# Where the matmul operands lie in SBUF: a 32-byte offset between stationary and moving tiles in a transformer block

## The chip, the cores and the metric

The kernel runs on one core of one Trainium2 chip. The metric is device time in microseconds (us) for one execution of the whole program; lower is better. Engines are named as in the profile: PE is TensorE (matmuls), PEld its weight loads, DVE VectorE, ACT ScalarE, POOL GpSimd, SP SyncE, which issues most DMAs. A matmul has a *stationary* operand (loaded into the array ahead of the matmul, the PEld rows) and a *moving* operand (streamed through it); both are read from SBUF, the result goes to PSUM.

## The reference

One layer of a streaming encoder on x of shape (1, 1024, 1024), float32:

```python
x = x + 0.5 * swiglu(rmsnorm(x, ffn1_norm), ffn1_w_gate, ffn1_w_up, ffn1_w_down)   # D_FF = 2816
h = rmsnorm(x, mix_norm); p = h @ w_in
#   A: gMLP spatial gating (8 groups x 64), B: gated DeltaNet (4 heads x 128), chunks of 64
x = x + concat(A, B) @ w_out
x = x + 0.5 * swiglu(rmsnorm(x, ffn2_norm), ffn2_w_gate, ffn2_w_up, ffn2_w_down)
y = rmsnorm(x, final_norm)
# swiglu(x, g, u, d) = (silu(x @ g) * (x @ u)) @ d
```

## The kernel before, in words

**Precision.** Every large product is made from float32r matmuls. `split` (line 60) makes two tiles of a float32 tile: a rounded one, `h` (a cast on ACT), and the remainder, `l` (a subtraction on DVE). `mm3` (line 55) then issues three matmuls into one PSUM bank: h x h, h x l, l x h, with the third argument pair as the moving operand. Small products in the mixer are plain float32 matmuls, transposes too.

**The two FFNs** (`ffn`, line 173) use Winograd's form of Strassen's scheme: seven products in place of eight on half-size blocks. `Combos` (line 107) holds the transposed activations and their sums (B11, B21, B22, T1 to T4), made once per FFN; they are the moving operands. For each of the 22 chunks of 128 hidden columns, `load_gu` (line 182) loads the gate and up weights, makes the weight sums on POOL and splits them into seven tiles of the pool `gp` (tag `gsp`); these are the stationary operands. `gu` (line 246) runs 7 products x 4 slices x 3 matmuls = 84 matmuls with 512 moving columns, and DVE and ACT combine the results; the hidden activations go to DRAM. Chunk 0 is done without the scheme by `gu_plain` (line 230) in two halves of 256 columns; a quarter of its products has as moving operand the tile B12, which comes from `gp` like the weights.

**Down projection.** Three `group`s (line 309) do the same on hidden activations and down weights: `group(0, 1)` has one pair of chunks per block, the other two have two. POOL and DVE make the sums in the buffers `hx`; `unit` (line 303) splits a left and a right factor into one tile (tag `cmb` of the pool `bp`, three buffers), and `mms` (line 335) runs 24 matmuls on it: the left factor is stationary, the right one moving. DVE adds finished banks into the residual `x` or into `acc`. The generator keeps two units prepared ahead of the one that runs. The last pair of chunks, number 10, goes without the scheme (`pair`, line 407, and the loop at line 435): 96 matmuls, both operands in `cmb` tiles.

**The mixer** (`middle`, line 659) projects `hT`, the transposed normalized activations in `actT` tiles of the pool `ap`. `proj_steps` (line 833) has the weights (`wk`, pool `wp`) stationary and `hT` moving, 512 columns; `token_steps` (line 694) has `hT` stationary and the weights moving, 256 or 264 columns of a 256- or 272-column slice. The steps of these generators are woven between the small products of the DeltaNet scan. Then `w_out` (line 555) has the transposed mixer output `yT` (pool `ap`) stationary and the weights (tag `gsp`) moving, 256 columns.

**Layout of SBUF.** Tiles of a pool lie one after another in the order of first use, `bufs` of each tag, rounded up to 32 bytes; a pool begins where the one opened before it ends. The pools that live throughout are `cp` (constants), `sm` (small statistics, three buffers for each of 11 tags, four for `ms` and `rs`), `xp` and `ap`; `gp`, `qp`, `bp` or the mixer's pools follow, by stage. In bytes from the start of a partition, before: `cp` 16,512, `sm` 21,152, `xp` 22,464, `ap` 55,232, and 120,768 for the first pool of a stage. `half` is 32 bytes and `grow` 4,096, so `grow` begins at 17,056, 32 past a multiple of 64. All tiles that a matmul reads begin at a multiple of 64.

```python
u = bp.tile([P, 2, 2, 2, 512], F32R, tag="cmb", name="unit", bufs=3)          # line 304
mm3(ps[t], u[:, 0, 0, j, tsl], u[:, 1, 0, j, tsl], u[:, 0, 1, j], u[:, 1, 1, j], ...)   # line 339
```

Of the kernel before, what the change touches and what calls it, by code (L numbers as in the profile page):

```python
# [10 lines left out]
F32 = mybir.dt.float32  # L11
F32R = mybir.dt.float32r
# [5 lines left out]
P = 128  # L18
# [12 lines left out]
def block_kernel(ctx: ExitStack, tc, a, out):  # L31
    nc = tc.nc

    def pool(stack, name, bufs=1, space=None):
        kw = {} if space is None else {"space": space}
        return stack.enter_context(tc.tile_pool(name=name, bufs=bufs, reuse_waits="tile", **kw))


    cp = pool(ctx, "cp")
    sm = pool(ctx, "sm", 3)  # L40
    xp = pool(ctx, "xp", 8)
    ap = pool(ctx, "ap", 4)
    dr = pool(ctx, "dr", 1, DRAM)

    ident = cp.tile([P, P], F32, tag="ident", name="ident")
    half = cp.tile([P, 8], F32, tag="half", name="half")
    nc.vector.memset(half, -0.5)

    def bank(p, tag):
        return p.tile([P, 512], F32, tag=tag, name=tag)  # L50

    def mm(*args, **kw):
        nc.tensor.matmul(*args, **kw)  # L53

    def mm3(o, lh, ll, rh, rl, first, last, **kw):
        mm(o, lh, rh, start=first, stop=False, **kw)
        mm(o, lh, rl, start=False, stop=False, **kw)
        mm(o, ll, rh, start=False, stop=last, **kw)

    def split(h, l, src):  # L60
        nc.scalar.copy(h, src)  # L61
        nc.vector.tensor_tensor(l, src, h, op=ALU.subtract)  # L62

    def grow(name):
        g = cp.tile([P, D], F32, tag="grow", name="grow")
        nc.scalar.dma_start(g, a[name].to_broadcast([P, D]))
        return g

    def rpow(o, i, w):
        nc.gpsimd.tensor_tensor(o, i, half[:, :w], op=ALU.pow)  # L70
# [9 lines left out]
    def normed(xt, g, xn, junk=None):  # L80
        rs = rstd_of(xt, xn if junk is None else junk, D)
        nc.vector.scalar_tensor_tensor(xn, xt, rs, g, op0=ALU.mult, op1=ALU.mult)  # L82
        return xn
# [5 lines left out]
    def acts():  # L89
        return [[act_tile() for _ in range(2)] for _ in range(2)]  # L90
# [7 lines left out]
    def to_T(pp, blk, tt, dst):  # L98
        sl = slice(tt * P, tt * P + P)
        for q in range(2):  # L100
            pv = transposed(pp, lambda i: blk(q * 4 + i))
            nc.scalar.copy(dst[q][:, 0, :, sl], pv)  # L102
            nc.vector.tensor_tensor(dst[q][:, 1, :, sl], pv, dst[q][:, 0, :, sl], op=ALU.subtract)
# [65 lines left out]
    def together(*parts, n=None):  # L169
        for _ in islice(zip_longest(*parts), n):  # L170
            pass

    def ffn(cb, wgu, wd, ps, gp, qp, bp, start, emit, before={}):
# [127 lines left out]
                nc.sync.dma_start(x[:, 1, ks], wd[2 * q:2 * q + 2][:, :, dh * 512:dh * 512 + 512].rearrange("j p n -> p j n"))  # L301

        def unit(l, r):
            u = bp.tile([P, 2, 2, 2, 512], F32R, tag="cmb", name="unit", bufs=3)
            for i, s in enumerate((l, r)):
                split(u[:, 0, i], u[:, 1, i], s)
            return u

        def group(p0, m, first, last):
            n = 2 * m  # L310
# [24 lines left out]
            def mms(ps, u, first, last, evac):  # L335
                for t in range(4):
                    tsl = slice(t * P, t * P + P)
                    for j in range(2):
                        mm3(ps[t], u[:, 0, 0, j, tsl], u[:, 1, 0, j, tsl], u[:, 0, 1, j], u[:, 1, 1, j],
                            first and j == 0, last and j == 1, skip_group_check=True)  # L340
                    if evac is not None:
                        evac(t, ps[t])
# [27 lines left out]
            def p1(kp, ks):  # L370
                u = unit(x1[:, 0, ks], x1[:, 1, ks])
                s1, t1 = st[kp]
                sub(x1[:, 0, ks], s1, x1[:, 0, ks], eng=other)
                sub(x1[:, 1, ks], x4[:, 1, ks], t1)
                return u
# [18 lines left out]
            ps = None  # L394
            for f, pp, start, stop, ev in plan:
                for kp in range(m):
                    def prep(f=f, kp=kp):
                        return f(kp, slice(2 * kp, 2 * kp + 2))

                    def run(u, pp=pp, kp=kp, start=start, stop=stop, ev=ev):  # L400
                        nonlocal ps
                        if start and kp == 0:
                            ps = [bank(*pp) for _ in range(4)]
                        mms(ps, u, start and kp == 0, stop and kp == m - 1, ev if kp == m - 1 else None)
                    yield prep, run
# [15 lines left out]
        for prep, run in units:  # L421
            ahead.append((run, prep()))
            if len(ahead) > 2:
                r, u = ahead.pop(0)
                r(u)
        prep = pair(10)
        r, u = ahead.pop(0)
        r(u)
        w = [prep(0)]
        r, u = ahead.pop(0)  # L430
# [4 lines left out]
        for t in range(8):  # L435
            tsl = slice(t * P, t * P + P)
            for f in range(2):
                fs = slice(f * 512, f * 512 + 512)
                p = bank(*X)
# [12 lines left out]
    def psums(stack, n):  # L452
        return [pool(stack, f"ps{i}", k, PSUM) for i, k in enumerate(n)]
# [5 lines left out]
    def load_x(src, ts):  # L459
        xs = {}  # L460
        for t in ts:
            xs[t] = xp.tile([P, D], F32, tag="x", name="x")
            nc.sync.dma_start(xs[t], src[t])
        return xs
# [6 lines left out]
    with ExitStack() as f1:  # L471
        ps = psums(f1, (4, 4))
        gp = pool(f1, "gp")
        qp = pool(f1, "qp")
        bp = pool(f1, "bp")
        cb = Combos(g, qp, bp)

        def start1(f):
            def xi(i):
                return xs[i], xs[i + 4]  # L480

            uv = [cb.sums() for _ in range(2)]
            for j in range(2):
                for i in range(2):
                    normed(xi(i)[j], g, xi(i)[j], uv[i][j])
            def b12():
                return [f.gtile(F32R, "B12").rearrange("p s (k n) -> p s k n", k=2) for _ in range(2)]

            weights = f.load_gu(0, True)
            next(weights)  # L490
            b = b12()
            parts = [cb.blocks(i, f.X, xi(i), uv[i], b) for i in range(2)]
            together(*parts, n=2)
            together(*parts, weights, n=2)
            xs.update(load_x(xdram, (2, 3, 6, 7)))
            f.gu_plain(slice(0, 256), b)
            rest = xi(2) + xi(3)
            ms = sm.tile([P, 4], F32, tag="ssk", name="ms4")
            for i, x in enumerate(rest):
                nc.scalar.activation(f.gtile(F32, "junk").rearrange("p s n -> p (s n)"), x, AF.Square, accum_out=ms[:, i:i + 1])  # L500
            rs = sm.tile([P, 4], F32, tag="rk", name="rs4")
            nc.vector.tensor_scalar(rs, ms, 1.0 / D, EPS, op0=ALU.mult, op1=ALU.add)
            rpow(rs, rs, 4)
            for i, x in enumerate(rest):
                nc.vector.scalar_tensor_tensor(x, x, rs[:, i:i + 1], g, op0=ALU.mult, op1=ALU.mult)
            together(*parts)
            b = b12()
            parts = [cb.blocks(i, f.X, xi(i), cb.sums(), b, eng=nc.vector) for i in range(2, 4)]
            together(*parts, n=4)
            f.gu_plain(slice(256, 512), b)  # L510
            together(*parts)

        st = {}

        def after(xts):
            st["gm"] = grow("mix_norm")
            xts.update(load_x(xdram, range(8)))

        def to_mid(t, xt):
            nc.sync.dma_start(xd[t], xt)  # L520
            if t == 0:
                st["hT"] = acts()
                st["xn"] = bp.tile([P, 4, D], F32, tag="cmb", name="xn", bufs=3)
            xn = st["xn"][:, t % 4]
            normed(xt, st["gm"], xn)
            return lambda: to_T((ps[1], "ax"), lambda c: xn[:, c * P:(c + 1) * P], t % 4, st["hT"][t // 4])

        ffn(cb, a["f1gu"], a["f1wd"], ps, gp, qp, bp, start1, to_mid, {2: [after]})
        hT = st["hT"]

    g2 = grow("ffn2_norm")
    with ExitStack() as mid:
        ps_m, ps_a, ps_s = psums(mid, (3, 2, 1))
        wp = pool(mid, "wp")
        ep = pool(mid, "ep")
        ts = pool(mid, "ts")
        up = pool(mid, "up")
        tl = pool(mid, "tl")
        lv = pool(mid, "lv")
        kp = pool(mid, "kp")  # L540
        yblk = middle(tc, nc, a, locals())

    with ExitStack() as f2:
        ps = psums(f2, (4, 4))
        bp = pool(f2, "bp")
        gp = pool(f2, "gp")
        qp = pool(f2, "qp")
        order = ((0, 4, 1, 5), (2, 6, 3, 7))
        yT = acts()
# [741 lines left out]
```

## Time and profile before

| | |
|---|---|
| median of 3 runs | 1914.35 us (1913.04 to 1918.01) |
| the profiled execution's own time | 1916.1 us |
| its span | 1914.0 us |
| PE busy | 1812.0 us, 95% of the span, 9,759 matmuls |
| mean granted TensorE clock | 0.981 |

The span is the time from the first to the last instruction of one profiled execution. Matmuls overlap, and the end of each is modelled, so the mean duration of a matmul in a row is longer than the distance from one start to the next; the pace is read from a piece with a count, as its length divided by the number. The chain of waits follows the work back from the last instruction; its pieces give start, length, engine, tile and line. A row of a group gives the shapes, the number of instructions, their busy time, the mean of one, and the idle time before them with what ended it.

### The profile page before, as it was taken

To read this page: it belongs to the slowest core of one execution; us is meant where nothing else is said; L and a number is where in the kernel's file an instruction comes from. 1 tells how busy PE (TensorE), PEld (TensorE's weight loads), DVE (VectorE), ACT (ScalarE), POOL (GpSimd) and SP (SyncE) were. 2 spreads that over 40 slices of the span, in tenths; PEclk is the share of its full clock that TensorE was granted. 3 is DMA by queue.
4 is the path that set the end of the run, shared out by engine and by line. 5 is a ranking of instruction groups with operands and counts; after the bars stand their busy time and mean duration, and the time that the engine had idled before them with its cause. 6 is when DMAs were issued, how large, how long until landed. Compare 5 with 4: busy or idle time off the path is not lost.

```text
span 1914.0 us, 25049 instructions
## 1 busy us (share of the span) xinstructions
PE 1812.0 (95%) x9759; PEld 1542.0 (81%) x9759; DVE 1253.3 (65%) x1663; ACT 674.2 (35%) x1171; POOL 665.9 (35%) x477
## 2 busy tenths in 40 slices
PE   6999999999798899898999999999999999979888
PEld 5888888887687689797788989988888888768766
DVE  7655555557988984668755236655555555798896
ACT  6333232334233343432354434433333332323233
POOL 4322222224647802221132402242323222454681
PEclk9999999999899999999999999999999999999999
DMA  6222222225222224354432343323232323531312
GB/s 227 92 91 78 88 78 89 77 89 200 89 79 97 84 107 141 122 182 122 130 90 65 118 145 122 115 74 97 68 99 67 99 67 98 171 115 57 119 44 88
DMA packets 95815, 199.98 MB, mean 104 GB/s; under 512 B 23857, under 2 KB 39505, under 8 KB 95697
## 3 DMA queue, kind: packets, MB, share of 16 engines
q1 hardware_dynamic: 93200, 193.95, 30.7%
q10 hardware_dynamic: 2496, 4.44, 0.8%
q8 instruction: 76, 1.25, 0.3%
q14 instruction: 43, 0.34, 0.1%
HBM read 149.06 MB, written 49.30 MB: 104 GB/s over the span
## 4 chain that ended last, share of the span: by engine, by line
PE 71%; DVE 15%; POOL 4%; issue 4%; ACT 3%; DMA 2%; DVEq 0%; POOLq 0%; SPq 0%; ACTq 0%
PE mm L53 40%; PE ax L53 29%; DVE unit L62 6%; DVE x L347 1%; POOL hx L323 1%; DVE acc L852 1%; POOL s L192 1%; PE sd L53 1%; DMA graw<-in_f1gu_dram 1%; PE ax L95 1%; PE sc L53 1%; POOL rs L70 0%; POOL E L778 0%; DVE xn L82 0%; ACT actT L102 0%
## 5 line engine op out<-in xcount | busy, mean ns | idle before, releaser
L53 PE MATMUL mm<-unit 128*128 128x512 f32 x960 | 240.9, 412 | 49.7 <-DVE acc L351 25.8
L62 DVE TENSOR_TENSOR unit<-hx,unit 128x1024 fp32r<-128x1024 f32 x128 | 247.2, 1971 | 45.0 <-ACT unit L61 44.3
L192 POOL TENSOR_TENSOR s<-graw 128x512 f32<-128x512 f32 x84 | 108.5, 1292 | 466.7 <-DMA graw<-in_f1gu_dram 178.9
L53 PEld LDWEIGHTS mm<-unit 128*128 128x128 f32 x960 | 192.0, 201 | 96.6 <-issue 48.9
L62 DVE TENSOR_TENSOR gs<-s,gs 128x512 fp32r<-128x512 f32 x168 | 162.0, 966 | 142.5 <-ACT gs L61 141.7
L61 ACT CAST unit<-hx 128x1024 fp32r<-128x1024 f32 x128 | 128.5, 1050 | 260.9 <-PE mm L53 84.7
L53 PE MATMUL ax<-unit 128*128 128x512 f32 x912 | 211.0, 390 | 4.0 <-DVE unit L62 3.4
L61 ACT CAST gs<-s 128x512 fp32r<-128x512 f32 x168 | 100.2, 620 | 317.9 <-POOL s L192 213.7
L53 PEld LDWEIGHTS ax<-unit 128*128 128x128 f32 x912 | 170.6, 188 | 40.6 <-DVE unit L62 4.2
L53 PE MATMUL ax<-T,gs 128*128 128x512 f32 x792 | 183.1, 389 | 0.0
L53 PEld LDWEIGHTS ax<-T,gs 128*128 128x128 f32 x792 | 148.7, 188 | 30.8
L62 DVE TENSOR_TENSOR ga<-graw,ga 128x512 fp32r<-128x512 f32 x134 | 96.2, 719 | 114.0 <-ACT ga L61 113.7
L53 PE MATMUL mm<-B,ga 128*128 128x512 f32 (+1 forms) x864 | 166.3, 347 | 0.2 <-ACT B L118 0.2
L53 PE MATMUL mm<-T,gs 128*128 128x512 f32 x720 | 166.4, 389 | 0.0
L53 PEld LDWEIGHTS mm<-T,gs 128*128 128x128 f32 x720 | 135.2, 188 | 28.0
L53 PEld LDWEIGHTS mm<-B,ga 128*128 128x128 f32 x864 | 139.7, 194 | 19.5 <-ACT B L118 0.5
L53 PE MATMUL mm<-actT,wk 128*128 128x512 f32 x576 | 152.3, 407 | 1.8 <-ACT ev L713 1.8
L53 PE MATMUL mm<-wk,actT 128*128 128x256 f32 (+1 forms) x1152 | 147.9, 286 | 0.0
L53 PEld LDWEIGHTS mm<-wk,actT 128*128 128x128 f32 x1152 | 141.2, 191 | 0.4
L53 PE MATMUL ax<-B,ga 128*128 128x512 f32 x528 | 126.9, 389 | 0.0
L323 POOL TENSOR_TENSOR hx<-hx 128x1024 f32<-128x1024 f32 x40 | 126.8, 3201 | 0.0
L53 PEld LDWEIGHTS mm<-actT,wk 128*128 128x128 f32 x576 | 105.0, 191 | 21.4 <-ACT ev L713 2.0
(240 smaller groups left out, 2756.4 us busy)
## 6 DMA issues: line engine op xcount, KB each, us to landing
graw<-in_f1gu_dram SPq DMA_DIRECT2D x44, 512.0 KB, 4.3
graw<-in_f2gu_dram SPq DMA_DIRECT2D x44, 512.0 KB, 3.9
hd<-sg SPq DMA_DIRECT2D x42, 512.0 KB, 5.1
hx<-hd SPq DMA_DIRECT2D x40, 512.0 KB, 6.3
hx<-in_f1wd_dram SPq DMA_DIRECT2D x20, 512.0 KB, 6.8
hx<-in_f2wd_dram SPq DMA_DIRECT2D x20, 512.0 KB, 7.4
x<-in_x_dram SPq DMA_DIRECT2D x16, 512.0 KB, 6.1
graw<-in_wo_dram SPq DMA_DIRECT2D x16, 512.0 KB, 3.8
```

Source lines behind the costliest of these rows:

```text
L53: nc.tensor.matmul(*args, **kw)
L61: nc.scalar.copy(h, src)
L62: nc.vector.tensor_tensor(l, src, h, op=ALU.subtract)
L95: nc.tensor.transpose(ps[:, i * P:(i + 1) * P], blk(i), ident)
L192: nc.gpsimd.tensor_tensor(f, u, v, op=op)
L323: eng.tensor_tensor(o, u, v, op=op)
L347: nc.vector.scalar_tensor_tensor(xv, p, 0.5, xv, op0=ALU.mult, op1=ALU.add)
L852: nc.vector.scalar_tensor_tensor(acc, pad[:, j:j + 512], cw[:, blk, j:j + 1], acc, op0=ALU.mult, op1=ALU.add)
```

## The change

All float32r stationary operands are meant to begin 32 bytes past a multiple of 64 and the moving ones at a multiple. A new helper, `shift`, takes a 32-byte tile at the start of a pool, which pushes what follows by 32 bytes; it is called for `gp` and `qp` in the first FFN, `wp` in the mixer, and `gp` in the second FFN. `unit` takes one flat tile of 4,112 elements in place of 4,096, with the right (moving) factor at its start and the left (stationary) one from element 2,056. To make room and keep `xp` and `ap` at a multiple of 64, `half` takes 64 bytes, and `sm` has two buffers per tag instead of three. `pair` and B12 are as before, and no instruction is added or taken away.

```diff
-    sm = pool(ctx, "sm", 3)
+    sm = pool(ctx, "sm", 2)
...
-    half = cp.tile([P, 8], F32, tag="half", name="half")
+    half = cp.tile([P, 16], F32, tag="half", name="half")[:, :8]
     nc.vector.memset(half, -0.5)
+
+    def shift(p):
+        p.tile([P, 8], F32, tag="shift", name="shift")
...
         def unit(l, r):
-            u = bp.tile([P, 2, 2, 2, 512], F32R, tag="cmb", name="unit", bufs=3)
-            for i, s in enumerate((l, r)):
-                split(u[:, 0, i], u[:, 1, i], s)
+            t = bp.tile([P, 4112], F32R, tag="cmb", name="unit", bufs=3)
+            u = [t[:, o:o + 2048].rearrange("p (s j n) -> p s j n", s=2, j=2) for o in (2056, 0)]
+            for v, s in zip(u, (l, r)):
+                split(v[:, 0], v[:, 1], s)
             return u
...
-                        mm3(ps[t], u[:, 0, 0, j, tsl], u[:, 1, 0, j, tsl], u[:, 0, 1, j], u[:, 1, 1, j],
+                        mm3(ps[t], u[0][:, 0, j, tsl], u[0][:, 1, j, tsl], u[1][:, 0, j], u[1][:, 1, j],
...
         gp = pool(f1, "gp")
+        shift(gp)
         qp = pool(f1, "qp")
+        shift(qp)
         bp = pool(f1, "bp")
...
         wp = pool(mid, "wp")
+        shift(wp)
...
         gp = pool(f2, "gp")
+        shift(gp)
         qp = pool(f2, "qp")
```

## The prediction

> **What bounds the kernel now.** I read the page's busy times first, then the chain of work that ended last, then the stretches of the span side by side, and last the timeline, for the pace of single matmuls. The page:
>
> ```profile
> span 1914.0 us, 25049 instructions
> PE 1812.0 (95%) x9759; PEld 1542.0 (81%) x9759; DVE 1253.3 (65%) x1663; ACT 674.2 (35%) x1171; POOL 665.9 (35%) x477
> PE 71%; DVE 15%; POOL 4%; issue 4%; ACT 3%; DMA 2%; DVEq 0%; POOLq 0%; SPq 0%; ACTq 0%
> ```
>
> TensorE is 71% of the chain that sets the end. The busy times by stretch (span, PE, weight loads, DVE, ACT, POOL; the granted clock third from the end) say where:
>
> ```profile
> 95.00:455.00 360.00, 360.00 (x1590) 298.20 (x1589) 196.77 (x263) 111.37 (x187) 92.50 (x73) 1.00 0.29 92
> 455.00:523.00 68.00, 55.04 (x228) 43.98 (x226) 64.29 (x51) 24.07 (x27) 43.90 (x16) 0.92 0.39 133
> 523.00:587.00 64.00, 64.00 (x270) 52.72 (x271) 50.95 (x45) 21.06 (x22) 22.86 (x8) 0.95 0.32 110
> 587.00:651.00 64.00, 50.24 (x212) 40.19 (x210) 62.81 (x36) 22.05 (x25) 61.08 (x22) 0.93 0.19 72
> 1090.00:1250.00 160.00, 154.74 (x1277) 151.42 (x1276) 82.22 (x143) 65.91 (x131) 37.32 (x38) 1.00 0.38 129
> 1296.00:1655.00 359.00, 359.00 (x1586) 297.36 (x1585) 196.32 (x263) 110.97 (x187) 92.18 (x72) 1.00 0.28 91
> ```
>
> The two gate/up loops (95 to 455, 1296 to 1655) are all TensorE at full clock, with DVE at 55%. In the down projection (455 to 700, and again from 1655) PE fills one stretch, and DVE and POOL fill those on both sides of it.
>
> Then the pace. The first two rows below are pieces of the chain of waits (start, us, engine, instructions); the others are timeline rows (start of the first to the modelled end of the last):
>
> ```profile
> 304.96 19.04 PE mm L53 x84
> 1191.87 43.31 PE mm L53 x361
> 727.93 6.95 PE L53 MATMUL mm<-wk,actT 128*128 128x264 f32 x56
> 1185.16 1.91 PE L95 MATMUL ax<-ident,x 128*128 128x128 f32 x16
> 1014.30 1.06 PE L53 MATMUL ax<-Z,ks 128*128 128x128 f32 x8
> ```
>
> A 512-column float32r matmul comes every 19.04 / 84 = 226.7 ns, a 256-column one every 43.31 / 361 = 120.0 ns. The difference, 106.7 ns for 256 columns, is 0.4167 ns per column; so each of them pays 120.0 - 106.7 = **13.3 ns beside its columns**, the same for both widths. This fixed part is all that the change can touch. Two things say that it need not be there. The plain float32 rows run at twice the time per column: 128 columns are 106.7 ns, and starts are about 109 ns apart for transposes ((1.91 - 0.27) / 15) and 112 ns for the products ((1.06 - 0.27) / 7), so they pay 2.3 and 5.3 ns, although each has a 128-column load of its own too. And it isn't constant: the 264-column matmuls come every (6.95 - 0.28) / 55 = 121.3 ns, where 264 x 0.4167 + 13.3 would be 123.3; they pay 11.3. Theirs are the only float32r operands whose slices start at steps other than whole multiples of 512 bytes (272 columns apart, 1,088 bytes). A cost that is paid once per load and gives way where the addresses or the phase shift looks like the weight load and the moving stream meeting in SBUF.
>
> **The change part by part.** It issues no instruction more or less, nothing is moved on a queue, and no DMA changes size. What changes is where tiles lie. Worked from the tile sizes: before, every matmul tile starts at a multiple of 64. After, `half` adds 32 bytes, `sm` loses 11 x 32 = 352, `xp` starts at 22,144 (64 x 346), `ap` at 54,912 (64 x 858), and the first pool of a stage at 120,448 (64 x 1,882); there a `shift` tile pushes `gp` or `wp` to 32 past, and a second one in the first FFN brings `bp` back. A `unit` slot is 16,448 bytes (64 x 257), its stationary half at 8,224 (64 x 128 + 32).
>
> So of the float32r matmuls these get operands in opposite halves of 64 bytes: all 3,528 of gate/up (2 x 21 x 84), 1,680 of the 1,872 on units, the projections (576, 960 and 192), 768 of the output projection, and three quarters of the 384 of `gu_plain`. For the 960, 192 and 768 the roles are swapped: there the stationary operand is `actT` at a multiple, and the weights move. Unchanged are the 192 on pair 10 (both operands from `bp`) and the quarter of `gu_plain` that reads B12 (both from `gp`).
>
> ```profile
> L53 PE MATMUL mm<-unit 128*128 128x512 f32 x960 | 240.9, 412 | 49.7 <-DVE acc L351 25.8 <-DVE x L347 19.9 <-ACT acc L354 2.4
> L53 PE MATMUL ax<-unit 128*128 128x512 f32 x912 | 211.0, 390 | 4.0 <-DVE unit L62 3.4 <-DVE x L443 0.6
> L53 PE MATMUL mm<-actT,wk 128*128 128x512 f32 x576 | 152.3, 407 | 1.8 <-ACT ev L713 1.8
> L53 PE MATMUL mm<-wk,actT 128*128 128x256 f32 x960 | 123.6, 286 | 0.0
> L53 PE MATMUL mm<-wo,actT 128*128 128x256 f32 x768 | 94.2, 284 | 2.7 <-DVE wo L62 2.7
> L53 PE MATMUL mm<-wk,actT 128*128 128x264 f32 x192 | 24.5, 286 | 0.0
> ```
>
> *What one is worth.* No row shows a float32r matmul with operands in opposite halves. At most the whole 13.3 ns goes. By the transposes 2.3 ns stay (a gain of 11.0), by the plain products 5.3 (a gain of 8.0); by the 264-column row only 2.0 are gained; nothing excludes zero, nor a loss. I take **9.5 ns**, the middle of the two float32 rows, since these are the instructions of the same array with the same 128-column load. The Trainium skill, "TensorE: Matmul & The Clock Gate", section "Back-to-back issue gap", gives a matmul N / 2.4 + 2.5 ns. This trace has 13.3 in place of the 2.5; a fall to that figure would be 10.8 ns each, an estimate 8 us below mine.
>
> *How many lie on the path.* Gate/up: all 3,528, PE has no gap there. Output projection: these pieces, less 96 of `gu_plain`, make 741; of those 96, 72 change, and with some 62 of the 82 in the first two pieces `gu_plain` brings 134.
>
> ```profile
> 42.18 4.53 PE mm L53 x29
> 47.59 6.36 PE mm L53 x53
> 1127.89 57.44 PE mm L53 x476
> 1191.87 43.31 PE mm L53 x361
> ```
>
> Projections: in the chain between 700 and 1250 us
>
> ```profile
> by line: PE mm L53 48.5%; PE ax L53 10.6%; DVE acc L852 3.5%; issue 3.5%; PE sd L53 2.4%; PE sc L53 1.8%; POOL E L778 1.7%; ACT actT L102 1.6%; POOL brs L70 1.3%; DVE wk L62 1.3%; PE sq L53 1.2%; DVE aT L899 1.2%; DMA grb<-grd 1.1%; DVE X L
> ```
>
> 0.485 x 550 = 267 us are such matmuls; less the two pieces above 166 are left, of 576 x 0.2267 + 960 x 0.120 + 192 x 0.121 = 269 us that they run: 62% of 1,728 is 1,070. Down projection, per FFN:
>
> ```profile
> 485.51 8.58 PE mm L53 x24
> 494.08 5.45 PE ax L53 x24
> ...
> 522.98 14.03 PE mm L53 x48
> 537.00 10.88 PE ax L53 x48
> 547.88 21.76 PE mm L53 x96
> 569.64 16.34 PE ax L53 x72
> ...
> 651.05 13.24 PE mm L53 x48
> 664.28 25.86 PE ax L53 x114
> ```
>
> 48 + 264 + 48 + 18 (the other 96 of the 114 are pair 10) = 378, twice 756. Together 3,528 + 741 + 134 + 1,070 + 756 = **6,229**, and 6,229 x 9.5 ns = 59 us.
>
> *What the shorter matmuls uncover.* A gate/up chunk would take 84 x 217.2 = 18.2 us; DVE's share of it rises from 55 to 57%, and the seven weight tiles come free one product at a time, so a product's tile has the other six products, some 16 us, to be split again. Nothing is late next there. In the down projection DVE has 51 us of work in 64 of the full stretch, so the gain holds; the stretch after it is POOL's (61 of 64) and starts earlier by what is gained, since its first split waits for a matmul. If it didn't hold there and half of the projections' gain were lost too, 913 x 9.5 = 9 us less.
>
> *The rest, costed at nothing.* Two `sm` buffers: the statistics in `mix` are used up by DVE, in order, before the tile after next is written; `rq` is free after the last POOL product of its half's scan, half a stage before its slot is wanted; `br2` and `bw` after the DVE products of a half, a whole projection before. If that cover failed, each wait would be some POOL step as in the first row here, 24 of them 13 us. Tiles at 32 past a multiple for DVE, ACT and the DMAs: `grow` lies so already (17,056 = 64 x 266 + 32), and reading it beside `x` costs 1,285 ns for 1,024 columns against 1,254 for a product whose tiles are all at multiples; 30 ns on an engine with slack.
>
> ```profile
> 691.00 0.56 POOL rs L70
> ...
> L62 DVE TENSOR_TENSOR wk<-raw,wk 128x1024 fp32r<-128x1024 f32 x22 | 27.6, 1254 | 7.5 <-ACT wk L61 7.5
> L82 DVE SCALAR_TENSOR_TENSOR o<-x,rs,grow 128x1024 f32<-128x1024 f32 x7 | 9.0, 1285 | 1.3 <-POOL rs L70 0.7
> ```
>
> The profiled execution took 1916.1 us (span 1914.0), so 1916.1 - 59.2 = 1856.9; the median lies 1.75 below that execution, which makes **1855 us**.
>
> **The rivals.** *Only part of it.* The swapped arrangement gains nothing: 1,920 matmuls drop out, on the path 741 + 0.62 x 1,152 = 1,455, and 6,229 - 1,455 = 4,774 x 9.5 = 45 us, 1869 us. Or DVE and POOL take back what isn't gate/up or output projection: 4,269 x 9.5 = 41 us, 1874. Or a matmul falls only as far as the 264-column ones show: 6,229 x 2.0 = 12 us, 1902. For it: that row. Against: the pace is the same to 0.1 ns at two widths, as when every load meets the stream in the same way, which one shift should undo as a whole.
>
> *Nothing.* The 13.3 ns are the array's own price for a float32r weight load; the time stays at 1914. For: the same at 512 and 256. Against: 11.3 at 264. This is what the Trainium skill says: by "SBUF — State Buffer", section "Who interferes with whom", PE has two read ports, one for the moving operand and one for the loads, independent of each other, and never waits on anyone; the 264-column row speaks against it.
>
> *Slower.* Today's arrangement is the one that mostly misses, and opposite halves are those that meet: the load then stalls the stream at each 64 bytes of both. Its place is the gate/up loops first of all. The smallest price is the swing seen, 2.0 ns: 6,229 x 2.0 = +12 us, 1926; twice today's fixed part would be 83 us more, 1997. It decides from 0.9 ns per matmul on. For it: all operands lie alike now, so no row says which relation is the bad one. Against: 13.3 is the largest fixed part of all rows.
>
> **How the numbers follow.** My forecast 0.52, with its own range 1843 (11.0 ns, 68.5 us) to 1872 (8.0 ns and the loss of 9 us); part of it 0.21; nothing 0.14; slower 0.13. Below about 0.3%, 5.7 us, a measurement of this kernel tells no change. Faster 0.74, within 0.3% 0.13, slower 0.13. The range runs from 1838 (somewhat over 11 ns) to 1915, which leaves out the slower case, half of no change, and the 1833 of a fixed part that is gone altogether.
>
> **What would show it.** Right: chain pieces of 84 matmuls at 18.1 to 18.4 us in place of 19.04; 256-column ones near 110 to 112 ns; the last 96 of each FFN still at 226.7 ns, a control inside the kernel; DVE and POOL group means unchanged. Wrong at the price: 84 still in 19.0, or more. Wrong at the path: pace as forecast, but PE idle before `unit` or in the projections grown by what was gained. Wrong on the buffers: new waits ahead of `rq`, `rk` or `bw` rows.

## The result and the profile after

The changed kernel takes 1939.97 us (median of four, 1934.68 to 1942.35) against 1914.34 us, the median of four for the kernel before: a ratio of 1.0127, 95% interval 1.0102 to 1.0152. It is **slower by 1.3%**, and the forecast of 1855 us had the wrong sign. The profiled execution is the fastest of the four, 1934.7 us; the lines below are its own.

The page after, first lines and the shares of the chain by engine:

```profile
span 1932.8 us, 25057 instructions
PE 1840.9 (95%) x9759; PEld 1536.9 (80%) x9759; DVE 1255.7 (65%) x1663; ACT 673.6 (35%) x1171; POOL 658.2 (34%) x477
PE 75%; DVE 13%; issue 4%; POOL 3%; ACT 3%; DMA 2%; DVEq 0%; POOLq 0%; SPq 0%; ACTq 0%
```

PE's share of the chain rose from 71% to 75%, and its busy time by 29 us with the same 9,759 matmuls; DVE, ACT and POOL have the times of before within 1.2%. So matmuls came more slowly. The chain of waits after (start, length, engine, instructions), at the places that divide the span:

```profile
96.88 19.61 PE ax L57 x84
116.49 19.60 PE mm L57 x84
...
449.72 16.82 PE ax L57 x72
...
675.70 26.57 PE ax L57 x114
...
1101.85 22.43 PE mm L57 x192
...
1200.33 42.70 PE mm L57 x361
...
1282.70 19.60 PE mm L57 x84
...
1655.44 16.83 PE ax L57 x72
```

and the same pieces before, as far as they haven't been shown:

```profile
95.53 19.04 PE ax L53 x84
...
438.25 16.33 PE ax L53 x72
...
1092.71 23.05 PE mm L53 x192
...
1276.34 19.31 PE mm L53 x84
...
1638.36 16.33 PE ax L53 x72
```

Three readings. A 512-column matmul comes every 19.60 / 84 = **233.3 ns**, 6.6 more than before. A 256-column one comes sooner: 22.43 / 192 = 116.8 ns against 120.1, and 42.70 / 361 = 118.3 against 120.0. And the ends of these pieces give the account: the first gate/up loop starts 1.4 us later and ends 12.0 later (466.54 against 454.58), so it loses 10.6; the first down projection loses 0.2 (702.27 against 690.14 is 12.1); the stretch from there to the second loop gains 5.8 (its piece starts at 1282.70 against 1276.34, 6.4 late), which is mostly not the placement's, as the second experiment shows; the second gate/up loop loses 11.2 (1672.27 against 1654.69, 17.6 late); the rest makes it 18.8 at the end of the span. The two gate/up loops lose 21.8 us, more than the 18.8 of this execution and most of the 25.6 us between the medians.

### The profile page after: what moved, and what is told of

Read it like the earlier page. It is cut to its first block, busy times and chain, and to the rows that moved or that the text cites. A ratio compares the mean times of both kernels' runs of the same rounds, so it can differ in the third digit from the quotient of the medians.

```text
span 1932.8 us, 25057 instructions
## 1 busy us (share of the span) xinstructions
PE 1840.9 (95%) x9759; PEld 1536.9 (80%) x9759; DVE 1255.7 (65%) x1663; ACT 673.6 (35%) x1171; POOL 658.2 (34%) x477
## 4 chain that ended last, share of the span: by engine, by line
PE 75%; DVE 13%; issue 4%; POOL 3%; ACT 3%; DMA 2%; DVEq 0%; POOLq 0%; SPq 0%; ACTq 0%
PE mm L57 41%; PE ax L57 31%; DVE unit L66 5%; POOL hx L328 1%; DVE x L352 1%; PE ax L99 1%; PE sd L57 1%; PE sc L57 0%; DVE xn L86 0%; DMA graw<-in_f1gu_dram 0%; ACT actT L106 0%; ACT unit L65 0%; POOL s L196 0%; DVE E L785 0%; POOL rs L74 0%
## 5 line engine op out<-in xcount | busy, mean ns | idle before, releaser
L66 DVE TENSOR_TENSOR unit<-hx,unit 128x1024 fp32r<-128x1024 f32 x128 | 242.9, 1938 | 47.9 <-ACT unit L65 47.5
L57 PE MATMUL ax<-unit 128*128 128x512 f32 x912 | 216.4, 396 | 3.7 <-DVE unit L66 3.2
L65 ACT CAST unit<-hx 128x1024 fp32r<-128x1024 f32 x128 | 128.1, 1046 | 262.1 <-PE mm L57 85.3
L57 PE MATMUL ax<-T,gs 128*128 128x512 f32 x792 | 188.7, 396 | 0.0
L57 PE MATMUL mm<-T,gs 128*128 128x512 f32 x720 | 171.6, 396 | 0.0
```

## The experiments

### Sweep of placements

A kernel of nothing but matmuls. `st` and `mv` are one stationary and one moving float32r tile, `s` and `m` the offsets in elements of 4 bytes:

```python
for _ in range(12):
    p = ps.tile([P, 512], F32, tag="mm", name=name)[:, :n]
    for k in range(4):
        lh, ll = (st[:, s + i * 512 + k * P:s + i * 512 + k * P + P] for i in range(2))
        rh, rl = (mv[:, m + i * 2048 + k * 512:m + i * 2048 + k * 512 + n] for i in range(2))
        nc.tensor.matmul(p, lh, rh, start=k == 0, stop=False)
        nc.tensor.matmul(p, lh, rl, start=False, stop=False)
        nc.tensor.matmul(p, ll, rh, start=False, stop=k == 3)
```

> This kernel leaves out the whole block: it copies x to the output and runs 144 float32r matmuls in the order of mm3 for each of 24 placements at 512 columns and 24 at 256 columns, from one stationary and one moving tile. Theory H (halves of 64 bytes: what counts is whether the two operands lie in the same half): at 512 columns 226.7 ns for stationary offsets 0, 64, 128, 192, 256, 320, 384, 448, and about 233 ns for 32, 96, 160, 224, 480; both at 32: 226.7. Theory S (same place in 512 bytes: the weight load runs beside the moving stream without loss only where both lie at the same place of a period of 512 bytes): 226.7 ns at 0 and both at 16 or 32, and 232 to 234 ns at every other one, 64 and 384 too. Theory A (absolute: a stationary operand off a multiple of 64 costs, wherever the moving one is): both at 32 is as slow as stationary 32. At 256 columns the after profile has 120.0 ns in the same place and 116.7 to 118.5 in four others; H expects 120.0 again at multiples of 64, S expects it at 0 only.

Mean distance from one start to the next in ns, worked from the starts of the 144 matmuls of each placement (offsets in bytes; the moving operand at 0 except in the last three columns):

```
stationary      0     16     32     64    128    192    224    256    320    384    448    480 | both 16  both 32  moving 32
512 columns  226.7  233.3  233.3  233.3  232.4  228.9  233.3  226.7  233.4  232.4  228.9  233.3 |  230.0    227.0      233.4
256 columns  120.0  118.3  118.3  113.3  118.6  117.8  117.8  119.9  117.8  118.7  117.8  117.8 |  118.4    120.0      116.7
```

H falls: 64 and 320 are multiples of 64 and are as slow as 32. A falls: with both at 32 the pace is that of both at 0. S stands in part, at 512 columns: the period is 256 bytes, not 512 (0 and 256 agree, 64 and 320, 128 and 384, 192 and 448), and a common offset of 16 isn't harmless. Nor is the same place the only fast one: of the six stationary offsets that the table leaves out, 496 comes every 226.7 ns as well, where S expected 232 to 234; the others (4, 8, 48, 96 and 160) come every 230.7 to 234.3. What matters most for the kernel: of these placements, **the same place is the fastest at 512 columns and among the slowest at 256**.

### Two buffers without the shift

```diff
-            u = [t[:, o:o + 2048].rearrange("p (s j n) -> p s j n", s=2, j=2) for o in (2056, 0)]
+            u = [t[:, o:o + 2048].rearrange("p (s j n) -> p s j n", s=2, j=2) for o in (2048, 0)]
...
-        shift(gp)
...
-        shift(qp)
...
-        shift(wp)
...
-        shift(gp)
```

(`t` goes back to 4,096 elements.)

> The changed kernel without the shift tiles and with the unit halves back at a multiple of 512 bytes apart; two buffers in the pool of small tiles and the 64-byte half tile stay. If the loss is the placement alone: the time of before, 1914 us, within 0.3%, gate/up pieces of 84 matmuls at 19.04 us. If two buffers cost something: the part of the 25 us that stays, with new waits at rq, rk, bw or brs, and gate/up at 19.04 all the same.

1914.8 us against 1912.72, ratio 1.0009 (0.9987 to 1.0031). From its chain of waits:

```profile
96.29 19.04 PE ax L54 x84
```

The second `sm` buffer and the larger `half` cost nothing that can be measured; the loss comes with the shifts. The trace of this kernel also takes most of the 5.8 us gained between the FFNs away from the placement. Worked from the starts, it is 401.5 us from the last `unit` matmul of the first FFN to the last projection matmul before, 398.0 after, and 397.2 here without any shift; the output projection behind it takes 107.9, 107.4 and 109.2 us. Of the six traces of the whole block two have 401.5 us for the first stretch, the others 397.0 to 398.0, with and without shifts; why isn't shown.

### Shifts of 64 bytes

```diff
-        p.tile([P, 8], F32, tag="shift", name="shift")
+        p.tile([P, 16], F32, tag="shift", name="shift")
...
-            u = [t[:, o:o + 2048].rearrange("p (s j n) -> p s j n", s=2, j=2) for o in (2056, 0)]
+            u = [t[:, o:o + 2048].rearrange("p (s j n) -> p s j n", s=2, j=2) for o in (2064, 0)]
```

> The changed kernel with shifts of 64 bytes in place of 32 (the unit halves at 0 and 64 past a multiple too), so that all operands lie at multiples of 64 again. Theory H: the time of before, 1914 us, gate/up pieces 19.04 us. Theory S: as slow as the changed kernel, 1930 to 1945 us, gate/up pieces 19.5 to 19.7 us.

1929.17 us, ratio 1.0079 (1.0059 to 1.0099): slow, with every operand at a multiple of 64, so H falls in the kernel too. Its chain has both gate/up loops:

```profile
96.54 19.51 PE ax L57 x84
116.05 19.51 PE mm L57 x84
...
1304.39 19.20 PE ax L57 x84
1323.59 19.20 PE mm L57 x84
```

The second loop is nearly as fast as before. There `bp` lies ahead of `gp`, its slots are 16,448 bytes apart, and most products end up a multiple of 256 bytes apart; worked from the program's addresses and the starts, those come every 227.5 ns, the ones 128 or 192 apart every 232.6 and 229.9. In the first loop the offsets are 64, 128 and 192, and the means 233.1, 231.6 and 228.9. That is the sweep's order, found again in the kernel.

### Only the gate/up weights shifted

```diff
-            t = bp.tile([P, 4112], F32R, tag="cmb", name="unit", bufs=3)
-            u = [t[:, o:o + 2048].rearrange("p (s j n) -> p s j n", s=2, j=2) for o in (2056, 0)]
+            t = bp.tile([P, 4096], F32R, tag="cmb", name="unit", bufs=3)
+            u = [t[:, o:o + 2048].rearrange("p (s j n) -> p s j n", s=2, j=2) for o in (2048, 0)]
...
-        shift(wp)
```

> The changed kernel with two of its parts taken back: the pool of projection weights isn't shifted and the unit halves are 2,048 elements apart in slots of 16,384 bytes; what stays is the shift of the gate/up weights, which moves the output projection's weights too. Theory S says that the loss is the number of 512-column matmuls on the chain times some 6.6 ns: 3,528 x 6.6 = 23 us from gate/up, less 741 x 2 = 1.5 us that the output projection gains, so 1913 + 22 = 1935 us, with gate/up pieces of 19.5 to 19.7 us and unit matmuls back at 226.7 ns. The rival, that the loss sits in the down projection or the mixer (DVE or POOL slowed by tiles off a multiple of 64): 1913 to 1920 us, gate/up pieces under 19.2.

1931.24 us against 1911.78, ratio 1.0110 (1.0080 to 1.0141). With the gate/up weights alone shifted, 19.5 us are lost, of the 25.6 that the whole change loses, and the gate/up pieces are as slow as there; the rival, that the loss sits in the down projection or the mixer, falls as the main cause. (The shift moves the output projection's weights too.) From its chain:

```profile
96.35 19.59 PE ax L57 x84
...
449.03 16.81 PE ax L57 x72
...
578.50 16.34 PE ax L57 x72
...
672.80 25.86 PE ax L57 x114
```

The unit pieces are back at 16.34 / 72 and 25.86 / 114, 226.9 ns. This also shows what the units cost, by one execution of each kernel. From the end of the gate/up loop to the end of the piece of 114 it takes 698.66 - 465.84 = 232.8 us here, 235.7 with the whole change (702.27 - 466.54), and 235.6 before (690.14 - 454.58). So slower units cost 2.9 us in the first FFN, and a slower gate/up loop gives 2.7 us back at the start of the down projection; I take it that more of DVE's and POOL's preparation is done when the loop ends. In the second FFN it is less: from the first `unit` matmul to the last, worked from the starts, 247.8 us here, 250.1 with the whole change and 248.6 before, which makes 2.3 and 0.8.

### Finer offsets, narrower loads

The same loop, with

```diff
-    for _ in range(12):
-        p = ps.tile([P, 512], F32, tag="mm", name=name)[:, :n]
+    for _ in range(6):
+        p = ps.tile([P, 512], F32, tag="mm", name=name)[:c, :n]
...
-            lh, ll = (st[:, s + i * 512 + k * P:s + i * 512 + k * P + P] for i in range(2))
+            lh, ll = (st[:, s + i * 512 + k * P:s + i * 512 + k * P + c] for i in range(2))
```

and other placements; `c`, the columns of weights, is 128 but for four of them.

> This kernel leaves out the block as the first sweep did; 72 matmuls for each placement: all pairs of a moving offset 0, 4, 8, 16 or 24 and a stationary offset 0 to 240 in steps of 16 at 512 columns, more moving offsets at 256 columns, and loads of 64 and of 32 columns of weights. In the first sweep 512 columns took 226.7 ns at 0 and 256 and never less, and 256 columns between 113.3 and 120.0. Theory M (meeting: what is paid beside the columns is the load's reads getting in the way of the stream's, so a narrower load pays less): beside 213.3 ns, a load of 64 columns pays about 6.7 and one of 32 about 3.3 in the same place, against 13.3 for 128. Theory F (a fixed price for each float32r weight load, with losses on top in some placements): 13.3 ns for 64 and 32 columns too. Both: a period of 256 bytes, no placement at 512 columns under 226.5 ns; if one is under 222 ns, the 13.3 ns are no floor and that placement can be taken into the kernel. At 256 columns, moving 16 again 113.3 ns, and the repeat of it at the end the same within 0.3 ns if the placement alone sets the pace.

```
512 columns, means over 16 stationary offsets (0 to 240):   lowest   highest
  moving at 0                                                226.7     234.3
  moving at 4                                                235.0     240.0
  moving at 8                                                231.1     235.6
  moving at 16                                               226.7     233.4
  moving at 24                                               231.8     234.9
stationary load of 64 columns, same place and 32 past:       229.9     231.6
stationary load of 32 columns, same place and 32 past:       231.7     239.4
256 columns, moving at 16, stationary at 0: 113.3; the same again at the end: 116.6
```

None of the 80 placements at 512 columns goes under 226.7 ns: the 13.3 ns are the least that any of them pays, and there is no placement to be taken into the kernel there. Theory M falls as put, since narrower loads pay more, not less. And the repeat at 256 columns isn't within 0.3 ns, so the placement alone doesn't set that pace.

Nor does it always at 512 columns, which I had overlooked. The moving operand at 0 and the stationary one at 16 gave 233.3 ns in the first sweep, behind the placement at 8, and 226.7 here, behind the one at 0; both at 16 gave 230.0 and 233.2. And with the moving operand at 16, the 226.7 belong to stationary offsets of 32, 48, 112 and 208, none of them the same place. What holds in all sweeps, behind the first matmuls of each, is narrower: both at 0, 256 apart, or both at 32 came every 226.7 to 228.2 ns.

### What came before, other widths, bfloat16

The loop of the second sweep with another list of placements, and a second pair of tiles:

```diff
+    stb = cp.tile([P, 1280], BF16, tag="stb", name="bst")
+    mvb = cp.tile([P, 4352], BF16, tag="mvb", name="bmv")
...
+        S, M, z = (stb, mvb, 2) if kind == "b" else (st, mv, 4)
+        s, m = s // z, m // z
...
+            pairs = [(lh, rl), (lh, rh), (ll, rh)] if kind == "o" else [(lh, rh), (lh, rl), (ll, rh)]
```

> Leaves out the block like the other sweeps; 72 matmuls each. Three rounds of nine placements that follow one another, then eight widths in the same place and 32 past it, then the three products of mm3 in another order, then bfloat16 operands at 512 and 256 columns with stationary offsets 0, 16, 32, 64 and 128. Theory L (locked: a run of equal matmuls falls into a repeating pattern, and which one depends on the placement and on how it was entered): at 512 columns in the same place always 226.7 ns, whatever came before; at 256 columns with the moving operand 16 past, 113.3 ns after some predecessors and 116.6 after others, the same in the three rounds. Theory P (placement alone): each of the nine the same in all rounds and after every predecessor. On the price: if the 13.3 ns at 512 columns come with every float32r load, other widths in the same place pay 6.7 to 13.3 ns beside their columns; if it is a price of weight loads of any type, bfloat16 pays it too; if bfloat16 pays 2 to 3 ns and placement doesn't move it, both the price and the sensitivity belong to float32r.

Timeline rows (start, length to the modelled end of the last, shapes, count); the pace is the distance from one row's start to the next row's, divided by 72. In the names, `full` and `half` are 512 and 256 columns, the number is the offset (of the moving operand in `halfsixteen` and `halfsixtyfour`, else of the stationary one), the last letter the round; `wide` gives the number of columns, with the stationary operand in the same place or 32 past; `brain` is bfloat16, with the stationary offset in units of 16 bytes:

```profile
36.18 8.71 PE L82 MATMUL halfsixteena<-mv,st 128*128 128x256 f32 x72
44.73 16.50 PE L82 MATMUL fullzeroa<-mv,st 128*128 128x512 f32 x72
61.07 8.71 PE L82 MATMUL halfsixteenfromfulla<-mv,st 128*128 128x256 f32 x72
69.61 16.95 PE L82 MATMUL fullthirtytwoa<-mv,st 128*128 128x512 f32 x72
86.41 16.49 PE L82 MATMUL fullzerofromoffa<-mv,st 128*128 128x512 f32 x72
102.74 16.91 PE L82 MATMUL fullonetwentyeighta<-mv,st 128*128 128x512 f32 x72
119.48 8.32 PE L82 MATMUL halfsixteenfromoffa<-mv,st 128*128 128x256 f32 x72
127.64 8.64 PE L82 MATMUL halfsixtyfoura<-mv,st 128*128 128x256 f32 x72
...
228.06 8.32 PE L82 MATMUL halfsixteenfromoffb<-mv,st 128*128 128x256 f32 x72
236.22 8.64 PE L82 MATMUL halfsixtyfourb<-mv,st 128*128 128x256 f32 x72
...
353.27 8.15 PE L82 MATMUL wideonetwentyeightsame<-mv,st 128*128 128x128 f32 x72
361.25 8.20 PE L82 MATMUL wideonetwentyeightoff<-mv,st 128*128 128x128 f32 x72
369.29 8.23 PE L82 MATMUL wideoneninetytwosame<-mv,st 128*128 128x192 f32 x72
377.37 8.20 PE L82 MATMUL wideoneninetytwooff<-mv,st 128*128 128x192 f32 x72
385.40 10.75 PE L82 MATMUL widethreetwentysame<-mv,st 128*128 128x320 f32 x72
396.00 10.72 PE L82 MATMUL widethreetwentyoff<-mv,st 128*128 128x320 f32 x72
...
460.87 15.76 PE L82 MATMUL widefoureightysame<-mv,st 128*128 128x480 f32 x72
476.46 15.53 PE L82 MATMUL widefoureightyoff<-mv,st 128*128 128x480 f32 x72
491.83 16.01 PE L82 MATMUL widefourninetysixsame<-mv,st 128*128 128x496 f32 x72
507.68 16.48 PE L82 MATMUL widefourninetysixoff<-mv,st 128*128 128x496 f32 x72
523.99 16.51 PE L82 MATMUL widefiveofoursame<-mv,st 128*128 128x504 f32 x72
...
590.06 15.71 PE L82 MATMUL brainfullzero<-bmv,bst 128*128 128x512 bf16 x72
605.61 15.70 PE L82 MATMUL brainfullone<-bmv,bst 128*128 128x512 bf16 x72
621.15 15.70 PE L82 MATMUL brainfulltwo<-bmv,bst 128*128 128x512 bf16 x72
...
667.77 8.02 PE L82 MATMUL brainhalfzero<-bmv,bst 128*128 128x256 bf16 x72
675.63 8.02 PE L82 MATMUL brainhalfone<-bmv,bst 128*128 128x256 bf16 x72
```

Theory L holds, though not with its 116.6. At 512 columns the same place runs at 226.9 and 226.8 ns, whether 256-column matmuls or displaced ones ran before. At 256 columns the moving operand 16 past gives 118.7 ns after the first two predecessors and 113.3 after the one 128 past, and the other two rounds repeat it. The order of the three products changes nothing at 512 columns: with h x l first, the same place gives 227.5 ns and 32 past it 233.3.

The widths show what I had misread. Matmuls of 128 and of 192 columns come every 7.98 / 72 = 110.8 and 8.08 / 72 = 112.2 ns: not 64 columns' worth of 27 ns apart, but the same. The columns don't set that pace; I take it to be that of the weight loads, which all of these have alike; no run times a load alone. A 256-column matmul has 106.7 ns of columns (0.417 ns each, by bfloat16's two widths: (216.0 - 109.2) / 256) and, if that is so, a load of some 111 behind it, so at 120.0 it pays up to 9 ns over its load; a 512-column one has 213.3 ns of columns and pays 13.3 over those, a 320-column one (133.3) some 13.9, at 10.60 / 72 = 147.2 in the same place. Displacement doesn't cost at every width either: at 480 columns the same place is the slower one, 15.59 / 72 = 216.5 against 213.5 ns, and at 496 the faster one, 220.1 against 226.5. Bfloat16 comes every 216.0 and 215.8 ns at 512 columns and 109.2 at 256, some 2.5 ns beside its columns, and so at all five offsets tried: both the price and the sensitivity to placement belong to float32r here.

### One placement for the 256-column projections

On the kernel with two buffers and no shift, weights that move through 256 columns lie 16 bytes on:

```diff
-    def load_w(src):
-        raw = wp.tile([P, src.shape[-1]], F32, tag="raw", name="raw", bufs=2)
+    def load_w(src, past=0):
+        n = src.shape[-1]
+        raw = wp.tile([P, n], F32, tag="raw", name="raw", bufs=2)
         nc.sync.dma_start(raw, src)
-        s = wp.tile([P, 2, src.shape[-1]], F32R, tag="wk", name="wk", bufs=4)
+        past = past if n == 1024 else 0
+        s = wp.tile([P, 2 * n + past], F32R, tag="wk", name="wk", bufs=4)[:, past:].rearrange("p (s n) -> p s n", s=2)
...
-        ws = [load_w(s).rearrange("p s (k n) -> p s k n", k=4) for s in srcs]
+        ws = [load_w(s, 4).rearrange("p s (k n) -> p s k n", k=4) for s in srcs]
```

> The second kernel of this study (two small buffers, no shift) with one placement of its own: the weights that move through 256 columns in the projections to token-major lie 16 bytes on, so 960 matmuls change; all 512-column ones stay in the same place. In the sweeps such matmuls took 113.3 or 116.6 ns in place of 120.0. Theory S: 62% of 960 on the chain x 3.4 to 6.7 ns is 2 to 4 us off the time of before, 1909 to 1911 us where before is 1912 to 1913; the rows of these matmuls come every 113 to 117 ns, gate/up pieces stay at 19.04. The rival: the pace is broken up by the small matmuls woven between, and the time is that of before within 0.1%.

1914.91 us against 1914.54, ratio 0.9995 (0.9980 to 1.0009). From its chain:

```profile
1087.93 22.42 PE mm L54 x192
```

The pace did change, 116.8 ns in place of 120.1. The expected gain of 2 to 4 us would be a ratio of 0.9990 to 0.9979; the interval holds nearly all of that, and no gain as well, so the time decides nothing. The traces show no gain in the mixer: from the last `unit` matmul to the last projection matmul it is 397.1 us, against 397.2 in the kernel with two buffers and no shift, one execution each.

## Why the prediction was wrong

**What failed first: the reading of the 13.3 ns.** The step "each of them pays 13.3 ns beside its columns, the same for both widths" took two things for one because their sizes agree. At 256 columns other placements come down to 113.3 ns, 6.6 beside the columns, and the pace of 111 ns that narrower matmuls keep to, the loads' as I take it, lies above the 106.7 of the columns; so 120.0 minus the columns is no price of a matmul. (The 0.4167 ns per column, worked from the same difference, happens to be right, as bfloat16 shows.) At 512 columns 13.3 is what the best of all placements tried still pays. So "all that the change can touch" could only grow.

**The rows that made the price.** I took 9.5 ns from plain float32 rows, "the same array with the same 128-column load". Their starts, 109 and 112 ns apart for 128 columns, are the pace of any float32r matmul of 128 or 192 columns too (110.8 and 112.2 ns in the sweep). So they show neither twice the time per column nor a price beside the columns, and say nothing on what a load does to a longer stream. The measured value is **-6.6 ns per 512-column matmul** and +1.7 to +3.3 per 256-column one. The 264-column row, which I read as a cost that gives way when the addresses shift, is a matmul near that pace of 111 ns; at 256 columns the placements don't rank as they do at 512.

**"Which one shift should undo as a whole."** The pace that is the same to 0.1 ns was read as a constant collision. But regularity tells nothing of that kind: in the sweeps the fastest pace repeats to the nanosecond (226 and 227 ns from start to start), and so does the slowest (240 each time, moving 4 and stationary 128 past).

**The placement.** "Opposite halves of 64 bytes" isn't the quantity; the distance modulo 256 bytes comes closer, though it doesn't fix the pace alone, as the second sweep shows. I had also overlooked what the 16,448-byte slots do: matmul operands in `bp` end up not only 32 past, but 96, 160 or 224. That broke my control: the last 96 matmuls of each FFN, both operands at multiples of 64 in two slots, and so 128 bytes past a multiple of 256 apart, were to stay at 226.7 ns and come every 26.57 / 114 = 233.1. The other part that was to stay, B12 with its weights (both at 32), does: 119 to 120 ns, worked from its starts, where the rest of `gu_plain` comes at 117 to 119.

**What held.** The path, in the main. Gate/up: of the 3,528 matmuls, 254 at the heads of the two loops ran before 95.53 and 1276.34. There "PE has no gap" was wrong: the chain goes through weight transfers, POOL and DVE, as in the 4.45 us of a transfer of `graw` at 64.95. The other 3,274 times the measured 6.6 ns make 21.6 us, and the loops lost 21.8. Units: 378 per FFN and the 96 of pair 10, times 6.6, make 3.1 us; the comparison above gives 2.9 and 2.3. What the 256-column matmuls gained can't be read from the stages: the output projection is 0.5 us shorter than before, and the mixer's 3.6 us come without any shift too. In the down projection "the gain holds" missed that the preparation at its start depends on how long the loop before it ran, 2.7 us the other way. The rest costed at nothing was nothing: two buffers 1.0009, and the large groups of DVE and ACT have their means (`gs` 966 and 967 ns, ACT on `unit` 1,050 and 1,046), though one group of ten on DVE, `unit<-s,unit`, went from 2,844 to 3,292. Two sums were slips that decided nothing: 6,229 x 11.0 ns gives 1846 us, not 1843, and the whole 13.3 gives 1832, not 1833.

**The rivals.** *Slower* was the right one, and right in that the old arrangement is the good one and the gate/up loops lose first. Its opposite halves are not the quantity: 64 past is as slow as 32, 233.3 ns each. Its price of 2.0 ns and 1926 us was too small by a factor of three at 512 columns, and its 13.3 too large. *Nothing*, with the Trainium skill's "SBUF — State Buffer", section "Who interferes with whom", by which the two read ports of PE are independent and PE waits on nobody: for bfloat16 the sweep agrees (215.8 to 216.0 ns at five offsets), for float32r it doesn't (226.7 to 240.0 ns by placement), and the measurement decides. The Trainium skill's "TensorE: Matmul & The Clock Gate", section "Back-to-back issue gap", gives N / 2.4 + 2.5 ns as the gap of an isolated matmul; here bfloat16 with a load for each matmul meets it to 0.2 ns (215.8), and no float32r placement at 512 columns does.

**What stays open.** That moving the operands changes the pace is shown; why isn't. Whether the load and the stream get in each other's way at all, and where, no run shows; that a narrower load pays more argues against counting its bytes. What fixes which of several paces a placement falls into is open too. Why the four timed executions of the changed kernel lie up to 7.7 us apart isn't shown either; the profile is of the fastest of them.

## What to carry to other kernels

Before a constant part of a pace is called a loss that placement can remove, measure it at several widths and for another type: a few hundred matmuls of each kind in one kernel would have said here that no placement pays less than 13.3 ns at 512 columns. Keep the stationary and moving operands of float32r matmuls with 512 columns at the same place modulo 256 bytes and at a multiple of 32 (both at 16 were slow), and look after slot sizes as much as pool starts; 3% of each matmul hangs on it. Don't carry this over to other widths untried: at 256 and 480 columns the same place wasn't the fastest. And that a pace repeats to the nanosecond doesn't tell whether it is the best one or the worst.

## What the runs showed of the hardware that I had not expected

- Float32r matmuls of 128 and 192 columns run at the same pace, 110.8 and 112.2 ns: their columns alone would differ by 27 ns.
- At 512 columns the pace ranges from 226.7 to 240.0 ns by the operands' places, the slowest with the moving operand 4 bytes past (235.0 to 240.0).
- One placement can have more than one steady pace: at 256 columns 113.3, 116.6 or 118.7 ns with the moving operand 16 past, by what ran before; at 512 columns 233.3 or 226.7 with the stationary one 16 past.
- Loads of 64 and 32 columns of float32r weights don't make a 512-column matmul cheaper: 229.9 and 231.7 ns against 226.7 for 128.
